# Forming the down projection's weight differences in another stage

## The chip, the cores and the metric

The kernel runs on one core of one Trainium2 chip. The metric is device time in microseconds (us) of one execution. Before the change it is 1341.98 us, the median of three runs (1338.4, 1341.98 and 1343.84).

In the profile PE is TensorE's matmuls and PEld its weight loads, DVE is VectorE, ACT is ScalarE, POOL is GpSimd. SP is the engine whose queue issues all of this kernel's DMAs, one behind the other (SPq in the rows).

## The reference, cut to what matters

One decoder layer over 1024 tokens and 16 meta tokens, model width 1024, all float32: a norm, an input projection that feeds four differential-attention heads and four HGRN heads in parallel, an output projection, a norm, and then a feed-forward part with a short convolution, which matters here:

```
def conv_ffn(a, w_up, conv_w, conv_b, w_down):
    u = a @ w_up                                   # 1024 -> 2 x 2816
    u = conv over 3 tokens, channel by channel, + conv_b
    gate, up = jnp.split(u, 2, axis=-1)
    return (jax.nn.gelu(gate, approximate=True) * up) @ w_down   # 2816 -> 1024
```

## The kernel before, in words

**Number format.** Every matmul operand in float32 is split into a rounded high part and a remainder (`split`, L146: the high part is a cast on ACT, the remainder a subtraction on DVE or POOL), and a product takes three matmuls (high by high, high by low, low by high). So each weight block costs a load, a cast and a subtraction before PE can use it.

**Stages.** The kernel is one unrolled program. After the first norm come the attention and HGRN heads: for each head `dense` (L742) computes input projections on PE while `attn` (L612) or `hgrn_head` (L395) runs beside it; `interleave` (L59) writes PE's order out by hand from costs per step. The stretches of this stage alternate: attention of a head beside the projections of the same head's HGRN (tiles `pi_hf`, `pi_hq`, `pi_hi`, `pi_hg`), then that head's HGRN beside the projections of the next head's attention (`pi_dq`, `pi_dk`, `pi_dv`). The order on PE is thus fixed; the order on the other engines and on SP is set at build time by a scheduler, in which an instruction earlier in the program goes first among those that it takes to be ready. `tc.issue_after(ins)` keeps what is issued inside the block behind `ins` on the engine of `ins`. At run time each engine works through its own queue in order and waits on semaphores.

**Up projection** (L1258 to L1371). The 2816 gate and 2816 up channels are worked off in 22 pairs of 128 (channel tiles, `ft` 0 to 21). From tile 1 on each pair is a two-by-two block product in seven products instead of eight, for two halves of the tokens (`unit`, p = 0 and 1, 258 and 256 columns per block). One tile has seven steps j = 0 to 6; in each, both units do 12 matmuls. The banks `pa`, `pb` and `pc` are accumulated into, evacuated and accumulated into again: step 1 fills `pb` and DVE adds it to `x1` to make `u2` (L1319, shown as `u<-pb`), step 3 adds further products into the same `pb`, so PE must wait there until that evacuation is done; DVE then makes `u3` (also `u<-pb`, L1325) and `uu`, step 5 goes into `pb` again. After step 6, `gated` (L1272) convolves gate and up (`conv`, L1263: one ACT instruction and two DVE instructions with three operands each, tiles `c`), takes gelu on ACT, multiplies on POOL and stores the rows to a DRAM scratch `gsc`. Beside this, `prep` (L1083) makes the weights of the next tile, seven steps ahead: loads `ra`, sums `ws` on POOL, high parts `uh` on ACT, remainders `ul` on DVE or POOL. Tile 0 is done plainly, in eight products (`plain_unit`).

**Down projection** (L1374 to L1547). It too is a block product in seven products, over 11 row blocks k. Four of the seven take differences of the weights of `w_down`: with blocks 11, 12, 21, 22 of rows k and k + 11 and of the two column halves, they are 12 - 11, 22 - 12, 22 - (12 - 11) and 21 - (22 - 12 + 11). They are formed ahead of time and kept in a DRAM scratch `tsc`, and `w_in` (L1394) reads them back for products 5, 6, 7 and 4, which are not the first two in the order (1, 2, 5, 6, 3, 7, 4).

**The differences** are made by `down_sums` (L184), a Python generator. For each of 11 values of k it loads four blocks `wd` (128x512, 256 KB each) on SP, then makes four subtractions on DVE in place, each followed by a store to `tsc`: 44 loads, 44 subtractions, 44 stores. Its blocks sit in six buffers of the pool `wsp`, which later also serves the output projection's weights. `dense` calls it once for each third of an input-projection tile (L749), so the work is spread over the attention and HGRN heads.

**The inputs of the down projection.** Rows of `gsc` come back in tiles `gi` (`g_in`, L1389), in the pool `dn` under the tag `gk` with four buffers; ACT and DVE split them into `gh` and `gl`, four buffers each. `ahead` (L1445) asks for them three steps ahead of use, and `sums5` (L1403) asks for rows of the second half. In program order the requests for `gk` buffers are: steps 0, 1, 2, 3 of product 1, then `sums5(0)`, then steps 4, 5 and so on. The pool `dn` is opened before tile 1 (L1359), so these loads can be issued during the up projection.

Of the kernel before, what the change touches and what calls it, by code (L numbers as in the profile page):

```python
# [9 lines left out]
F32 = mybir.dt.float32  # L10
# [3 lines left out]
ALU = mybir.AluOpType  # L14
# [3 lines left out]
P = 128  # L18
# [6 lines left out]
NF = DFF // P  # L25
# [6 lines left out]
WN = [258, 256]  # L32
C0 = [0, 514]
FA, FH, FO = 840, 800, 740


def start(i):
# [21 lines left out]
def interleave(dense, sides, fill, lead=0):  # L59
    sides = list(sides)  # L60
    live = True

    def feed(budget):
        nonlocal live
        while live and budget > 0:
            c = next(dense, False)
            if c is False:
                live = False
            elif c is None:
                return  # L70
            else:
                budget -= c

    feed(lead)
    while sides:
        for s in list(sides):
            c = next(s, False)
            if c is False:
                sides.remove(s)
                continue  # L80
            feed(fill * (c or 1))
    feed(1e12)
# [3 lines left out]
def layer_kernel(ctx: ExitStack, tc: tile.TileContext, x, meta, table, lbl, gpre, gpost, win,  # L86
# [3 lines left out]
    V, A = Ordered(tc, nc.vector, state), Ordered(tc, nc.scalar, state)  # L90
    G = Ordered(tc, nc.gpsimd, state)
    T, SY = nc.tensor, nc.sync

    def pool(name, bufs, side="left", space=None):
        kw = {"side": side} if space is None else {"space": space}
        cm = tc.tile_pool(name=name, bufs=bufs, reuse_waits="tile", **kw)
        return cm, cm.__enter__()
# [35 lines left out]
    tsc = dp.tile([4, DFF // 2, 512], F32, tag="tsc", name="tsc")  # L133
# [43 lines left out]
    ws_cm, wsp = pool("wdsums", 6)  # L177
# [3 lines left out]

    last_load = []

    def down_sums():  # L184
        def load(k):
            with tc.issue_after(last_load[-1].ins):
                for nm, kk, half in (("11", k, 0), ("12", k, 1), ("22", k + NF // 2, 1), ("21", k + NF // 2, 0)):
                    b[nm] = wsp.tile([P, 512], F32, tag="wd", name=f"wd{nm}_{k}")
                    SY.dma_start(b[nm], wdown[P * kk: P * (kk + 1), 512 * half: 512 * (half + 1)])

        b = {}
        load(0)
        yield
        yield
        for k in range(NF // 2):
            for j, d, p_, q_ in ((0, "11", "12", "11"), (2, "12", "22", "12"), (1, "22", "22", "11"), (3, "21", "21", "22")):
                V.tensor_tensor(b[d], b[p_], b[q_], op=ALU.subtract)
                with tc.issue_after(last_load[-1].ins):
                    SY.dma_start(tsc[j][P * k: P * (k + 1)], b[d])
                yield  # L200
            if k + 1 < NF // 2:
                load(k + 1)
                yield

    wd_sums = down_sums()
    at_p_cm, ap_ = pool("attn", 1, "right")
    z_cm, zp = pool("pre", 2, "right")

    def load_m(m, name, where=None, bufs=4):
        return [load_split(win[m][:, 512 * c: 512 * (c + 1)], f"{name}_{c}", where, bufs) for c in range(2)]  # L210

    def proj_group(g, parts, name, evac):
        b0, b1 = GROUPS[g]
        t0, t1 = start(b0), start(b1 - 1) + P
        n = t1 - t0
        pt = ps_in(f"pi_{name}_{g}")
        for k in range(KD):
            yield from proj_step(pt[:, :n], parts, k, t0, t1, lambda: evac(g, b0, b1, t0, t1, pt[:, :n]))
# [134 lines left out]
    def carried():  # L353
        tails = list(carry)
        carry.clear()
        return tails
# [34 lines left out]
    def flush():  # L391
        while late:
            to_nat(*late.pop(0))
# [345 lines left out]
                yield from values(i + 1)  # L739
        carry.append(pend.pop("tail"))  # L740

    def dense(tiles, preload=None, side=iter(())):  # L742
        parts = preload
        for idx, (m, name, evac) in enumerate(tiles):
            if parts is None:
                parts = load_m(m, name)
            nxt = load_m(tiles[idx + 1][0], tiles[idx + 1][1]) if idx + 1 < len(tiles) else None
            for g in range(3):
                next(side, None)  # L749
                for step, c in enumerate(proj_group(g, parts, name, evac)):  # L750
                    if step == 8:
                        flush()
                    yield c
            parts = nxt

    t_a, tiles = attn_in(0)
# [177 lines left out]

    for h in range(HEADS):
        t_h, tiles_h = hgrn_in(h)
        interleave(dense(tiles_h, None, wd_sums), [attn(h, t_a)] + carried(), FA, 1500)
        if h < HEADS - 1:
            t_a, tiles_a = attn_in(h + 1)
            interleave(dense(tiles_a, None, wd_sums), [hgrn_head(t_h)] + carried(), FH, 1500)  # L940

    close(at_cm)
    wo_cm, wop = pool("wo", 7)
# [127 lines left out]
    def load_raw4(ft):  # L1071
        raws.clear()
        for nm, m, c in (("11", ft, 0), ("22", ft + NF, 1), ("21", ft + NF, 0), ("12", ft, 1)):
            raws[nm] = swp.tile([P, 512], F32, tag="ra", name=f"ra{ft}_{nm}", bufs=5)
            with tc.issue_after(wo0_loaded.ins):
                SY.dma_start(raws[nm], wup[m][:, 512 * c: 512 * (c + 1)])
# [6 lines left out]
    def prep(q):  # L1083
        ft, j = divmod(q, 7)
        if ft >= NF or q in made:
            return
        if j == 0:
            load_raw4(ft)
            src = raws["11"]
            w_sum("1", raws["21"], raws["22"], ALU.add)  # L1090
        elif j == 1:
            src = w_sum("2", sums["1"], raws["11"], ALU.subtract)
        elif j == 2:
            src = sums["1"]
        elif j == 3:
            src = w_sum("3", raws["11"], raws["21"], ALU.subtract)
        elif j == 4:
            src = raws["12"]
        elif j == 5:
            src = raws["22"]  # L1100
        else:
            src = w_sum("4", raws["12"], sums["2"], ALU.subtract)
        where = swp if q % 2 else wp
        hi = where.tile([P, 512], F32R, tag="wh", name=f"uh{q}", bufs=4)
        lo = where.tile([P, 512], F32R, tag="wl", name=f"ul{q}", bufs=4)
        split(hi, lo, src, G if j % 2 == 0 and j else V)
        made[q] = (hi, lo)
# [150 lines left out]
    marks = {}  # L1258

    def outputs(ft, p):  # L1260
        return [xup.tile([P, 2 * WN[0]], F32, tag=t, name=f"{t}{ft}_{p}") for t in ("ug", "uu")]
# [36 lines left out]
    def unit(ft, p, bank):  # L1298
        n = WN[p]
        nm = f"{ft}_{p}"  # L1300
        ug, uu = outputs(ft, p)
        x1, u2, u3 = (xup.tile([P, WN[0]], F32, tag=t, name=f"{t}_{nm}")[:, :n] for t in ("x1", "u2", "u3"))

        def mm(j, pt, first):
            hi, lo = made[7 * ft + j]
            th, tl = tt[p][j]
            for k in range(4):
                s = slice(P * k, P * (k + 1))
                T.matmul(pt, hi[:, s], th[:, k], start=(first and k == 0), stop=False, skip_group_check=True)  # L1309
                T.matmul(pt, hi[:, s], tl[:, k], start=False, stop=False, skip_group_check=True)  # L1310
                T.matmul(pt, lo[:, s], th[:, k], start=False, stop=(k == 3), skip_group_check=True)  # L1311

        pa = bank(f"pa{nm}")[:, :n]
        mm(0, pa, True)
        A.copy(x1, pa)
        yield
        pb = bank(f"pb{nm}")[:, :n]
        mm(1, pb, True)
        marks[ft, p] = V.tensor_tensor(u2, pb, x1, op=ALU.add)  # L1319
        yield  # L1320
        pc = bank(f"pc{nm}")[:, :n]
        mm(2, pc, True)
        yield
        mm(3, pb, False)
        V.tensor_tensor(u3, pb, x1, op=ALU.add)  # L1325
        V.tensor_tensor(uu[:, n:2 * n], pc, u3, op=ALU.add)
        yield
        mm(4, pa, False)
        A.copy(ug[:, :n], pa)
        yield  # L1330
        mm(5, pb, False)
        V.tensor_tensor(uu[:, :n], pb, x1, op=ALU.add)
        yield
        mm(6, pc, False)
        V.tensor_tensor(ug[:, n:2 * n], pc, u2, op=ALU.add)
        gated(ft, p, ug, uu)
        yield

# [20 lines left out]
    dn_cm, dn = pool("down", 4, "right")  # L1359
    next(p0)  # L1360
    for j in range(4, 7):
        prep(7 + j)
    for ft in range(1, NF):
        units = [unit(ft, p, ps_b) for p in range(2)]
        for j in range(7):
            prep(7 * (ft + 1) + j)
            for u in units:
                next(u)
            if (ft, j) == (1, 1):
                with tc.issue_after(marks[1, 1].ins):  # L1370
                    next(p1)  # L1371
# [10 lines left out]
    x1 = ep.tile([P, 4, 512], F32, tag="e0", name="x1")  # L1382
    u2 = ep.tile([P, 4, 512], F32, tag="e1", name="u2")
# [230 lines left out]
```

## Time and profile before

| what | value |
|---|---|
| median of the runs | 1341.98 us |
| the profiled execution | 1336.17 us |
| its span, first to last instruction | 1334.1 us |
| granted TensorE clock | 0.995 |
| attention and HGRN heads | about 50 to 580 us of the span |
| up projection, tiles 1 to 21 | about 683 to 1108 us |
| down projection | from 1108 us |

The profile has a page and views that answer questions on the trace. The page gives busy time and share of each engine. The stretch view gives busy time of each engine between two times. The view of one tile or of one line gives count, shortest, median and longest duration, and first and last start. The view of waits gives, for an engine and what it wrote, which instruction or DMA it waited for: total, times, longest. The order in time gives start, length, engine, line, operation, output and inputs, shapes and count; in brackets stand the idle time of the engine before that instruction and what ended it. Names in rows are the program's tile names without numbers. Since V, A and G are wrapped in `Ordered`, their instructions all show line L53. Tiles written `wd`, `gi`, `gl`, `ul` and `u` are those described above.

### The profile page before, as it was taken

To read this page: it belongs to the slowest core of one execution; us is meant where nothing else is said; L and a number is where in the kernel's file an instruction comes from. 1 tells how busy PE (TensorE), PEld (TensorE's weight loads), DVE (VectorE), ACT (ScalarE), POOL (GpSimd) and SP (SyncE) were. 2 spreads that over 40 slices of the span, in tenths; PEclk is the share of its full clock that TensorE was granted. 3 is DMA by queue.
4 is the path that set the end of the run, shared out by engine and by line. 5 is a ranking of instruction groups with operands and counts; after the bars stand their busy time and mean duration, and the time that the engine had idled before them with its cause. 6 is when DMAs were issued, how large, how long until landed. Compare 5 with 4: busy or idle time off the path is not lost.

```text
span 1334.1 us, 26146 instructions
## 1 busy us (share of the span) xinstructions
PE 1287.9 (97%) x10172; PEld 1187.0 (89%) x10172; DVE 911.1 (68%) x1531; ACT 692.0 (52%) x1635; POOL 432.3 (32%) x340
## 2 busy tenths in 40 slices
PE   7999999999999999998998999999999999999997
PEld 6899899989999998677888999999999998878875
DVE  7675657475746574647797687787787776697586
ACT  8465356535654665246665445444445444454453
POOL 5211212121212110334055666666666630010121
PEclk9999999999999999999999999999999999999999
DMA  5331343144311223686412222223222226954253
GB/s 208 123 129 62 116 153 116 56 141 134 111 56 54 82 85 127 194 258 230 144 54 83 95 88 72 74 94 103 87 81 72 82 86 211 326 181 166 88 205 118
DMA packets 99425, 164.99 MB, mean 124 GB/s; under 512 B 10035, under 2 KB 34899, under 8 KB 99302
## 3 DMA queue, kind: packets, MB, share of 16 engines
q1 hardware_dynamic: 99302, 163.32, 35.9%
q8 instruction: 80, 1.31, 0.4%
q14 instruction: 43, 0.35, 0.1%
HBM read 122.65 MB, written 40.63 MB: 122 GB/s over the span
## 4 chain that ended last, share of the span: by engine, by line
PE 46%; DVE 7%; issue 3%; ACT 3%; DMA 2%; POOL 2%; SPq 0%; DVEq 0%; POOLq 0%; ACTq 0%
PE pd L1460 5%; PE pd L1461 5%; PE pd L1459 5%; PE pb L1309 4%; PE pb L1311 4%; PE pb L1310 4%; PE pc L1309 2%; PE pa L1309 2%; PE pa L1311 2%; PE pa L1310 2%; PE pc L1310 2%; PE pc L1311 2%; PE py L982 1%; PE py L980 1%; PE py L978 1%
## 5 line engine op out<-in xcount | busy, mean ns | idle before, releaser
L1309 PE MATMUL pb<-t,uh 128*128 128x258 f32 x504 | 142.9, 284 | 7.7 <-DVE u L53 7.7
L1310 PE MATMUL pb<-t,uh 128*128 128x258 f32 x504 | 141.7, 281 | 0.0
L1311 PE MATMUL pb<-t,ul 128*128 128x258 f32 x504 | 141.5, 281 | 0.0
L1460 PE MATMUL pd<-wl,gh 128*128 128x512 f32 x308 | 122.0, 396 | 0.3 <-DVE wl L53 0.2
L1459 PE MATMUL pd<-wh,gh 128*128 128x512 f32 x308 | 121.6, 395 | 0.0
L1461 PE MATMUL pd<-wh,gl 128*128 128x512 f32 x308 | 121.6, 395 | 0.0
L53 DVE SCALAR_TENSOR_TENSOR c<-uu,cwt,c 128x514 f32<-128x514 f32 (+1 forms) x88 | 97.1, 1104 | 20.6 <-ACT c L53 19.9
L1309 PEld LDWEIGHTS pb<-t,uh 128*128 128x128 f32 x504 | 95.4, 189 | 9.2 <-DVE u L53 8.9
L53 POOL TENSOR_TENSOR c<-c,c 128x514 f32<-128x514 f32 (+1 forms) x44 | 63.4, 1441 | 122.6 <-ACT c L53 118.5
L1310 PEld LDWEIGHTS pb<-t,uh 128*128 128x128 f32 x504 | 95.5, 189 | 0.0
L1311 PEld LDWEIGHTS pb<-t,ul 128*128 128x128 f32 x504 | 95.2, 189 | 0.0
L1309 PE MATMUL pa<-t,uh 128*128 128x258 f32 (+1 forms) x336 | 95.2, 283 | 0.0
L1311 PE MATMUL pa<-t,ul 128*128 128x258 f32 (+1 forms) x336 | 95.0, 283 | 0.0
L1310 PE MATMUL pa<-t,uh 128*128 128x258 f32 (+1 forms) x336 | 94.8, 282 | 0.0
L1309 PE MATMUL pc<-t,uh 128*128 128x258 f32 (+1 forms) x336 | 94.4, 281 | 0.0
L1310 PE MATMUL pc<-t,uh 128*128 128x258 f32 (+1 forms) x336 | 94.0, 280 | 0.0
L1311 PE MATMUL pc<-t,ul 128*128 128x258 f32 (+1 forms) x336 | 93.7, 279 | 0.0
L53 DVE SCALAR_TENSOR_TENSOR c<-ug,cwt,c 128x514 f32<-128x514 f32 (+1 forms) x88 | 86.7, 986 | 2.0 <-ACT c L53 1.4
L53 POOL TENSOR_TENSOR ul<-ws,uh 128x512 fp32r<-128x512 f32 x42 | 61.0, 1453 | 41.1 <-ACT uh L53 36.6
L1460 PEld LDWEIGHTS pd<-wl,gh 128*128 128x128 f32 x308 | 57.7, 187 | 15.5 <-DVE wl L53 1.6
L1459 PEld LDWEIGHTS pd<-wh,gh 128*128 128x128 f32 x308 | 57.7, 187 | 14.1
L1461 PEld LDWEIGHTS pd<-wh,gl 128*128 128x128 f32 x308 | 57.7, 187 | 14.0
(372 smaller groups left out, 4119.4 us busy)
## 6 DMA issues: line engine op xcount, KB each, us to landing
ra<-in_wup_dram SPq DMA_DIRECT2D x88, 256.0 KB, 2.6
mp<-msc SPq DMA_DIRECT2D x23, 512.0 KB, 6.3
wd<-in_wdown_dram SPq DMA_DIRECT2D x44, 256.0 KB, 4.4
tsc<-wd SPq DMA_DIRECT2D x44, 256.0 KB, 2.8
wi<-tsc SPq DMA_DIRECT2D x44, 256.0 KB, 2.8
gi<-gsc SPq DMA_DIRECT2D x33, 256.0 KB, 3.9
wi<-in_wdown_dram SPq DMA_DIRECT2D x33, 256.0 KB, 3.2
gsc<-c SPq DMA_DIRECT2D x22, 257.0 KB, 2.1
```

The costliest lines, as they stand in the source:

```text
L53: ins = call(*args, **kw)
L978: T.matmul(py[:r], mh, hi, start=(first and k == ks[0]), stop=False)
L980: T.matmul(py[:r], mh, lo, start=False, stop=False)
L982: T.matmul(py[:r], ml, hi, start=False, stop=(last and k == ks[-1]))
L1309: T.matmul(pt, hi[:, s], th[:, k], start=(first and k == 0), stop=False, skip_group_check=True)
L1310: T.matmul(pt, hi[:, s], tl[:, k], start=False, stop=False, skip_group_check=True)
L1311: T.matmul(pt, lo[:, s], th[:, k], start=False, stop=(k == 3), skip_group_check=True)
L1459: T.matmul(py, gh[:, s], wh, start=(k == 0 and pr not in (3, 7)), stop=False, skip_group_check=True)
L1460: T.matmul(py, gh[:, s], wl, start=False, stop=False, skip_group_check=True)
L1461: T.matmul(py, gl[:, s], wh, start=False, stop=(k == NH - 1), skip_group_check=True)
```

## The change

The generator moves from the attention stage into the up projection's loop, and `dense` loses its `side`. In the new place its blocks no longer lie in `wsp` but in the four buffers of the tag `gk`. It is called from channel tile 6 on (`SUMS`), after steps 1, 3, 5 and 6 of each tile, each time inside `issue_after` of the last evacuation traced so far (`marks["last"]`, set at each evacuation in `unit`), which is that of the second token half in this step. A call issues either the four loads of a k or one subtraction with its store: 55 calls in all. The arithmetic is the same.

```
+SUMS = 6
...
-        interleave(dense(tiles_h, None, wd_sums), [attn(h, t_a)] + carried(), FA, 1500)
+        interleave(dense(tiles_h), [attn(h, t_a)] + carried(), FA, 1500)
...
-            interleave(dense(tiles_a, None, wd_sums), [hgrn_head(t_h)] + carried(), FH, 1500)
+            interleave(dense(tiles_a), [hgrn_head(t_h)] + carried(), FH, 1500)
...
-        marks[ft, p] = V.tensor_tensor(u2, pb, x1, op=ALU.add)
+        marks[ft, p] = marks["last"] = V.tensor_tensor(u2, pb, x1, op=ALU.add)
...
-        V.tensor_tensor(uu[:, n:2 * n], pc, u3, op=ALU.add)
+        marks["last"] = V.tensor_tensor(uu[:, n:2 * n], pc, u3, op=ALU.add)
...
-        V.tensor_tensor(uu[:, :n], pb, x1, op=ALU.add)
+        marks["last"] = V.tensor_tensor(uu[:, :n], pb, x1, op=ALU.add)
...
-        V.tensor_tensor(ug[:, n:2 * n], pc, u2, op=ALU.add)
+        marks["last"] = V.tensor_tensor(ug[:, n:2 * n], pc, u2, op=ALU.add)
...
+    def down_sums():
+        for k in range(NF // 2):
+            b = {}
+            for nm, kk, half in (("11", k, 0), ("12", k, 1), ("22", k + NF // 2, 1), ("21", k + NF // 2, 0)):
+                b[nm] = dn.tile([P, 512], F32, tag="gk", name=f"wd{nm}_{k}")
+                SY.dma_start(b[nm], wdown[P * kk: P * (kk + 1), 512 * half: 512 * (half + 1)])
+            yield
+            for j, d, p_, q_ in ((0, "11", "12", "11"), (2, "12", "22", "12"), (1, "22", "22", "11"), (3, "21", "21", "22")):
+                V.tensor_tensor(b[d], b[p_], b[q_], op=ALU.subtract)
+                SY.dma_start(tsc[j][P * k: P * (k + 1)], b[d])
+                yield
+
+    wd_sums = down_sums()
...
+            if ft >= SUMS and j in (1, 3, 5, 6):
+                with tc.issue_after(marks["last"].ins):
+                    next(wd_sums, None)
```

More of the change, by code (lines that the diff above doesn't have):

```diff
@@ L182, in layer_kernel @@
     last_load = []
[L184 to L205, printed above, removed]
     at_p_cm, ap_ = pool("attn", 1, "right")
@@ L740, in attn, with dense @@
         carry.append(pend.pop("tail"))
-    def dense(tiles, preload=None, side=iter(())):
+    def dense(tiles, preload=None):
         parts = preload
@@ L748, in dense @@
             for g in range(3):
-                next(side, None)
                 for step, c in enumerate(proj_group(g, parts, name, evac)):
```

## The prediction

> **What bounds the kernel now.** The page comes first: span and engine shares.
>
> ```profile
> span 1334.1 us, 26146 instructions
> PE 1287.9 (97%) x10172; PEld 1187.0 (89%) x10172; DVE 911.1 (68%) x1531; ACT 692.0 (52%) x1635; POOL 432.3 (32%) x340
> ```
>
> TensorE (PE) is busy nearly all the time and no matmul is added or removed, so the change can only move PE's idle time. Two stages matter: attention beside HGRN, which loses the 44 differences, and the up projection, which gets them. The view of one tile (count, min/median/max ns, first and last start) places the old work; the waits of VectorE (DVE) add total, times, longest.
>
> ```profile
> L53 DVE TENSOR_TENSOR wd<-wd,wd x44: 673/693/1716, 56.4 to 349.8; 128x512 f32<-128x512 f32 x44
> DVE wd L53 <- DMA wd<-in_wdown_dram: 8.7, 10, 1.5
> ```
>
> This stage contains its own comparison, since the last difference is at 349.8 us while a third HGRN head follows without any. Its bounds are the first matmuls of tiles dq and hf of successive heads; the stretch view gives length, then PE, PEld, DVE, ACT and POOL busy (and count), clock, DMA share, GB/s.
>
> ```profile
> L224 PE MATMUL pi_dq<-ahi,wh_dq x24: 287/334/441, 137.8 to 154.7; 128*128 128x384 f32 x16, 128*128 128x272 f32 x8
> L224 PE MATMUL pi_hf<-ahi,wh_hf x24: 287/334/439, 191.3 to 205.8; 128*128 128x384 f32 x16, 128*128 128x272 f32 x8
> L224 PE MATMUL pi_dq<-ahi,wh_dq x24: 287/334/440, 267.1 to 285.3; 128*128 128x384 f32 x16, 128*128 128x272 f32 x8
> L224 PE MATMUL pi_hf<-ahi,wh_hf x24: 287/336/439, 321.1 to 335.7; 128*128 128x384 f32 x16, 128*128 128x272 f32 x8
> L224 PE MATMUL pi_dq<-ahi,wh_dq x24: 287/333/441, 397.2 to 412.2; 128*128 128x384 f32 x16, 128*128 128x272 f32 x8
> L224 PE MATMUL pi_hf<-ahi,wh_hf x24: 287/334/439, 447.9 to 462.4; 128*128 128x384 f32 x16, 128*128 128x272 f32 x8
> 137.80:191.30 53.50, 50.31 (x732) 47.52 (x732) 33.89 (x67) 23.84 (x67) 10.44 (x12) 1.00 0.36 120
> 191.30:267.10 75.80, 74.11 (x506) 71.21 (x506) 46.41 (x108) 45.95 (x139) 12.62 (x11) 1.00 0.33 110
> 267.10:321.10 54.00, 50.34 (x732) 47.50 (x732) 34.83 (x67) 23.81 (x67) 11.01 (x12) 1.00 0.35 118
> 321.10:397.20 76.10, 74.17 (x506) 71.20 (x505) 46.11 (x108) 45.98 (x139) 12.62 (x11) 1.00 0.33 107
> 397.20:447.90 50.70, 50.13 (x733) 47.44 (x732) 28.54 (x59) 23.83 (x67) 9.86 (x12) 1.00 0.18 57
> ```
>
> The same PE work with 67 DVE instructions takes 53.5 and 54.0 us, and with 59 (eight differences fewer) 50.7. In the up projection the stretch view shows PE full, DVE idle 24.1 of 105 us:
>
> ```profile
> 830.00:935.00 105.00, 105.00 (x888) 105.00 (x887) 80.89 (x118) 51.04 (x92) 64.99 (x46) 1.00 0.26 90
> ```
>
> **The change part by part.** *(a) Attention stage, removal.* Heads 0 and 1 should take what head 2 takes: 53.5 - 50.7 + 54.0 - 50.7 = 6.1 us. The order in time of DVE in head 0 shows the mechanism: a difference stood 1.48 us for its load ahead of the chain that PE's small matmuls need.
>
> ```profile
> 145.38 0.69 DVE L53 TENSOR_TENSOR wd<-wd,wd 128x512 f32<-128x512 f32 x1 [1.48 <-DMA wd<-in_wdown_dram]
> 146.58 1.42 DVE L53 TENSOR_TENSOR wd<-wd,wd 128x512 f32<-128x512 f32 x2
> ```
>
> The two attention stretches lose only 1.7 and 1.9 us of PE each, with attention's own waits among them; I take nothing, at most 3.6 together. Term: -6.1, bounds -9.7 and 0.
>
> *(b) Buffers of tag gk.* Before, the first four inputs gi of the down projection came into these four buffers during channel tiles 1 to 4, and PE paid. In the order in time the bracket is the idle before and its releaser:
>
> ```profile
> 701.99 0.69 DVE L53 TENSOR_TENSOR gl<-gi,gh 128x512 fp32r<-128x512 f32 x1 [3.50 <-ACT gh L53]
> 715.11 0.39 PE L1309 MATMUL pb<-t,uh 128*128 128x258 f32 x1 [3.30 <-DVE u L53]
> 719.28 0.62 ACT L53 CAST gh<-gi 128x512 fp32r<-128x512 f32 x1 [3.47 <-DMA gi<-gsc]
> 721.53 0.39 PE L1309 MATMUL pb<-t,uh 128*128 128x258 f32 x1 [0.45 <-DVE u L53]
> 742.36 0.39 PE L1309 MATMUL pb<-t,uh 128*128 128x258 f32 x1 [0.46 <-DVE u L53]
> 763.19 0.39 PE L1309 MATMUL pb<-t,uh 128*128 128x258 f32 x1 [0.42 <-DVE u L53]
> ```
>
> ACT stands in its queue for a load of rows just stored, DVE behind ACT, PE behind the evacuation u: 3.30 + 0.45 + 0.46 + 0.42 = 4.6 us. After the change the first four difference inputs are earlier in the program and need no stored rows, so I expect them to hold the buffers from the start, and gi to follow the last difference in tile 19. That buffers of one tag go in program order is supported by the next gi loads:
>
> ```profile
> 917.72 0.33 SPq L1277 DMA_DIRECT2D gsc<-c  x1
> 920.27 1.75 SPq L1391 DMA_DIRECT2D gi<-gsc  x4
> ```
>
> They leave only after tile 11's store, although rows of tiles 4 to 6 were there long before: the fifth request in program order (L1405) needs row 11. So -4.6 goes. The same four casts and differences come back in tiles 19 to 21, on rows stored long before; I charge 1.0, an estimate (two of the small waits above, since no load waits for a store there), bounds 0 and 4.6 (all returns).
>
> *(c) Up projection, addition.* Each call follows the evacuations of step j = 1, 3, 5 or 6. Of the 55 calls 11 load and 44 subtract, through j = 5 of tile 19. The order in time of DVE, PE and POOL decides which cost something:
>
> ```profile
> 876.33 0.74 DVE L53 TENSOR_TENSOR u<-pb,x 128x258 f32<-128x258 f32 x2
> 877.37 0.29 PE L1309 MATMUL pb<-t,uh 128*128 128x258 f32 x1
> 896.71 0.75 DVE L53 TENSOR_TENSOR u<-pb,x 128x258 f32<-128x258 f32 x2
> 897.30 0.29 PE L1309 MATMUL pb<-t,uh 128*128 128x258 f32 x1
> 898.10 0.69 DVE L53 TENSOR_TENSOR ul<-ws,uh 128x512 fp32r<-128x512 f32 x1 [0.65 <-ACT uh L53]
> 903.75 0.87 DVE L53 TENSOR_TENSOR ul<-ra,uh 128x512 fp32r<-128x512 f32 x1 [2.53 <-ACT uh L53]
> 906.01 0.76 DVE L53 SCALAR_TENSOR_TENSOR c<-uu,cwt,c 128x514 f32<-128x514 f32 x1 [0.95 <-ACT c L53]
> 908.07 1.63 POOL L53 TENSOR_TENSOR ws<-ra,ra 128x512 f32<-128x512 f32 x1
> 911.62 0.42 DVE L53 TENSOR_TENSOR ug<-pc,u 128x256 f32<-128x256 f32 x1
> 913.53 1.58 POOL L53 TENSOR_TENSOR c<-c,c 128x514 f32<-128x514 f32 x1 [3.83 <-ACT c L53]
> 916.19 0.75 DVE L53 TENSOR_TENSOR u<-pb,x 128x258 f32<-128x258 f32 x2
> L53 DVE TENSOR_TENSOR ul<-ra,uh 128x512 fp32r<-128x512 f32 x11 | 10.4, 942 | 12.7 <-ACT uh L53 12.7
> ```
>
> A difference at j = 1 lies in the idle 0.65, one at j = 3 in the idle 2.53: I cost both at nothing; without that cover their 22 would cost as those below. From 906.01 to the pair u at 916.19 DVE has no idle left, and the differences of j = 5 and 6 fall into this run, ahead of u. PE needs the first u of the pair: it ends about half the pair in, 897.09 against PE's start at 897.30 (margin 0.21), and 876.70 against 877.37 (0.67); the margins alternate by tile. One at j = 5 comes about a microsecond after 906.01, where GpSimd (POOL) works; I price it like ul, 0.94 on average. One at j = 6 comes behind 911.62, in POOL's idle 3.83; I price it at 0.69, wd's median. Loads take calls 0, 5, 10 and so on, which leaves 8 tiles with both (four of each margin), three with j = 5 alone (one at 0.21), three with j = 6 alone (two at 0.21). PE's stall: both, 4 x (1.63 - 0.21) + 4 x (1.63 - 0.67) = 9.5; j = 5, 0.73 + 2 x 0.27 = 1.3; j = 6, 2 x 0.48 + 0.02 = 1.0. Term +11.8. Below, it could be nothing (order otherwise); above, with 1.716, wd's slowest, for all 22, 22 x 1.716 - 7 x 0.21 - 7 x 0.67 = 31.6. I take the ul price since ul has the same form in this stage.
>
> The moved DMAs: 44 loads and 44 stores on SP.
>
> ```profile
> wd<-in_wdown_dram SPq DMA_DIRECT2D x44, 256.0 KB, 4.4
> tsc<-wd SPq DMA_DIRECT2D x44, 256.0 KB, 2.8
> ```
>
> A new buffer costs a store and a load, 2.8 + 4.4 = 7.2 us; from a fourth difference to the next first one lie at least three steps of (897.30 - 877.37) / 7 = 2.85, so 8.5. Nothing to wait for, narrowly: were the load late by 1 us, the conv chain and u behind it on DVE would be too. On SP the weight loads ra stand behind these issues; a DMA share of 0.26 leaves room. Cost nothing.
>
> *Sum:* -6.1 - 4.6 + 1.0 + 11.8 = +2.1 us. The profiled execution took 1336.17 us (span 1334.1 and 2.1 around it), so 1338.3; the shown median is 1341.98, against which I forecast **1344.1**.
>
> **The rivals.** *Slower: the port.* GpSimd is busy 65 of 105 us here against 10 to 11 of 54 in the HGRN stretches, and ul's mean is 942 ns where the one at 898.10 took 0.69. If each difference in the run costs more, the term grows by 22 us for each us of price: at 1.52 and 0.94 for j = 5 and 6 (mean 1.23) it is 22 x 1.23 - 6.2 = 20.9, and the time 1341.98 - 9.7 + 20.9 = 1353.2. It is slower by 0.5% (6.7 us) from a mean of 1.03. Against it: the idle 3.83 of POOL when j = 6 comes. The Trainium skill, SBUF — State Buffer, section "Who interferes with whom", has the rule: a DVE instruction with two SBUF inputs and a GpSimd instruction that reads SBUF exclude each other for the whole instruction. By it a difference behind a GpSimd instruction pays most of that one too, and the sum would be nearer 1353; wd's median of 693 with a maximum of 1716 agrees that it happens, seldom in the stage with little GpSimd work.
>
> *Faster: the run takes nothing.* If the differences reach DVE only in its idle places (24.1 us of 105 are there), (c) is 0 and the time 1332.3. Against it: j = 5 and 6 come before the next u in the program.
>
> *It doesn't do what it says: gi keeps its buffers.* If gi is still fetched in tiles 1 to 4, (b) is 0: 1341.98 - 6.1 + 11.8 = 1347.7, and differences delayed beyond tile 19 would be next. The four loads at 920.27 speak against.
>
> **How the numbers follow.** Forecast 0.50, port 0.27, faster 0.16, gi kept 0.07. Half a per cent is about what a measurement of this kernel can tell from no change: 1335.3 to 1348.7. Forecast gives 0.46 within, 0.01 faster, 0.03 slower; the port 0.27 slower; the third 0.16 faster; the last 0.06 within, 0.01 slower: faster 0.17, same 0.52, slower 0.31. The range takes in both rivals' times with about a microsecond beyond: 1331 to 1355; the forecast's own is 1338 to 1350.
>
> **What would show it.** HGRN heads 0 and 1 at 50.7 us each; no gl in tiles 1 to 4 and none of the four PE waits there; PE waits on u at step 3 of tiles 7 to 20, some 0.3 to 1.4 us each, in alternation; wd at j = 1 and 3 in DVE's idle. It would be wrong if wd at j = 5 or 6 stands behind the next u, if DVE waits for wd loads (the spacing above), or if ACT waits for ra because SP stands at a wd issue.

## The result, and the profile after

The kernel after takes **1337.24 us** (median of 22 runs, 1331.78 to 1340.71), the kernel before 1340.45 us (22 runs, 1336.26 to 1347.05). The ratio is 0.9974 with a 95% interval of 0.9963 to 0.9985: faster by 0.26%, about 3.5 us by this ratio (the medians alone differ by 3.2). Forecast was 1344.1 us, slower by 2.1. The time lies in the stated range (1331 to 1355) and within the half per cent that the prediction called no change, but below the forecast's own range (1338 to 1350) and on the other side of no change: the sign was wrong.

First the page of the kernel after, span and engine shares. Without the generator at its top the kernel's lines have moved: L53 is L54 here, PE's L1309 is L1287, the loads of `gi` at L1391 are at L1386.

```profile
span 1336.4 us, 26161 instructions
PE 1292.8 (97%) x10172; PEld 1191.7 (89%) x10172; DVE 929.2 (70%) x1531; ACT 691.5 (52%) x1635; POOL 453.7 (34%) x340
```

Each of the five engines has as many instructions in this row as before, but DVE is busy 18.1 us longer (911.1 before) and POOL 21.4 us longer (432.3). The profiled execution took 1338.2 us, 2.0 more than that of before (1336.17), while the median is 3.2 less. So the first pair of traces shows where time moved, but not the whole sum; two more executions of before come below (number 8).

**Attention beside HGRN.** The first and the last of the six bounds (tile view of the kernel after), then its stretches between them (length, PE, PEld, DVE, ACT, POOL busy with counts, clock, DMA share, GB/s):

```profile
L203 PE MATMUL pi_dq<-ahi,wh_dq x24: 287/333/440, 137.3 to 152.3; 128*128 128x384 f32 x16, 128*128 128x272 f32 x8
...
L203 PE MATMUL pi_hf<-ahi,wh_hf x24: 287/334/439, 439.9 to 454.4; 128*128 128x384 f32 x16, 128*128 128x272 f32 x8
```

```profile
137.30:188.00 50.70, 50.13 (x733) 47.43 (x733) 28.55 (x59) 23.86 (x67) 9.86 (x12) 1.00 0.16 49
188.00:263.20 75.20, 73.54 (x505) 71.22 (x504) 42.41 (x100) 46.53 (x138) 12.57 (x11) 1.00 0.16 48
263.20:313.90 50.70, 50.13 (x733) 47.43 (x732) 28.55 (x59) 23.83 (x67) 9.86 (x12) 1.00 0.16 48
313.90:389.20 75.30, 73.64 (x505) 71.32 (x505) 42.45 (x100) 46.63 (x139) 12.55 (x11) 1.00 0.17 48
389.20:439.90 50.70, 50.13 (x733) 47.43 (x733) 28.55 (x59) 23.85 (x67) 9.86 (x12) 1.00 0.19 56
```

All three HGRN heads take 50.7 us now, as forecast, and the attention stretches also give 0.6 and 0.8 us, which I had priced at nothing. The projections that follow head 2's HGRN start 8.0 us earlier (447.9 before).

**Up projection.** One row each: the differences in their new place, and the time that PE waited for the evacuation `u` there (total, times, longest):

```profile
L54 DVE TENSOR_TENSOR wd<-wd,wd x44: 676/1382/1577, 786.5 to 1063.2; 128x512 f32<-128x512 f32 x44
PE pb L1287 <- DVE u L54: 10.1, 11, 4.4
```

A difference takes 1382 ns in the median instead of 693. The four waits that the prediction showed ahead of tile 5 are gone. In their place PE waits in the tiles with differences, and once for 4.4 us. The order in time around that one wait, in tiles 19 and 20:

```profile
1054.69 0.32 SPq L1386 DMA_DIRECT2D gi<-gsc  x1
1058.00 0.62 ACT L54 CAST gh<-gi 128x512 fp32r<-128x512 f32 x1 [3.36 <-DMA gi<-gsc]
1058.65 1.65 DVE L54 TENSOR_TENSOR gl<-gi,gh 128x512 fp32r<-128x512 f32 x1 [1.30 <-ACT gh L54]
1060.64 0.95 SPq L1386 DMA_DIRECT2D gi<-gsc  x2
...
1064.87 0.62 ACT L54 CAST gh<-gi 128x512 fp32r<-128x512 f32 x1 [2.71 <-DMA gi<-gsc]
...
1067.45 1.86 DVE L54 SCALAR_TENSOR_TENSOR c<-uu,cwt,c 128x510 f32<-128x510 f32 x1 [2.58 <-POOL ul L54]
...
1075.10 0.41 DVE L54 TENSOR_TENSOR u<-pb,x 128x258 f32<-128x258 f32 x1
1075.44 1.71 DVE L54 TENSOR_TENSOR gl<-gi,gh 128x512 fp32r<-128x512 f32 x1
1075.57 0.58 PE L1287 MATMUL pb<-t,uh 128*128 128x258 f32 x1 [4.37 <-DVE u L54]
1075.95 0.42 PE L1288 MATMUL pb<-t,uh 128*128 128x258 f32 x1
```

Read the brackets on ACT: it stood 3.36 and 2.71 us for loads issued only a few microseconds before. Those rows had been stored long ago; what was late is the issue of the load, behind the last differences, against the cast's place in ACT's queue. The conv on DVE came 2.58 us late behind that, and with it `u` and PE. (Its bracket names POOL's `ul`; the conv's own ACT instruction, behind the second of the two casts, ran from 1066.54 to 1067.35, 0.1 us before the conv.) After the wait the matmuls start 0.21 to 0.22 us apart instead of 0.12, and the granted clock of 1070 to 1080 us is 0.72.

The start of the same matmul, counted from the first instruction of the span, after minus before, in the first pair of traces and with a second execution of after (against the same execution of before):

| where | first pair | second execution of after |
|---|---|---|
| end of head 2's HGRN | -8.0 | -8.2 |
| start of the up projection | -9.4 | -8.6 |
| tile 6, before the first difference | -15.0 | -15.1 |
| tile 19 | -6.0 | -6.2 |
| start of the down projection | +1.5 | +0.4 |
| last matmul | +1.8 | -0.1 |

So the four terms are there: the attention stage about -8 to -9, the end of the `gi` waits -5.6 to -6.5, the differences +9, the return of `gi` +7.

### The profile page after: what moved, and what is told of

It is laid out like the page before. It is cut to its first block, busy times and chain, and to the rows that moved or that the text cites. A ratio compares the mean times of both kernels' runs of the same rounds, so it can differ in the third digit from the quotient of the medians.

```text
span 1336.4 us, 26161 instructions
## 1 busy us (share of the span) xinstructions
PE 1292.8 (97%) x10172; PEld 1191.7 (89%) x10172; DVE 929.2 (70%) x1531; ACT 691.5 (52%) x1635; POOL 453.7 (34%) x340
## 4 chain that ended last, share of the span: by engine, by line
PE 43%; DVE 11%; DMA 4%; issue 3%; ACT 3%; POOL 1%; SPq 0%; DVEq 0%; POOLq 0%; ACTq 0%
PE pd L1455 5%; PE pd L1456 4%; PE pd L1454 4%; PE pb L1287 4%; PE pb L1288 4%; PE pb L1289 4%; DVE c L54 3%; PE pa L1287 2%; PE pa L1289 2%; PE pa L1288 2%; PE pc L1287 2%; PE pc L1288 2%; PE pc L1289 2%; DMA gi<-gsc 1%; DMA xh<-in_x_dram 1%
## 5 line engine op out<-in xcount | busy, mean ns | idle before, releaser
L1287 PE MATMUL pb<-t,uh 128*128 128x258 f32 x504 | 145.8, 289 | 12.2 <-DVE u L54 12.1
L1288 PE MATMUL pb<-t,uh 128*128 128x258 f32 x504 | 143.5, 285 | 0.0
L54 POOL TENSOR_TENSOR c<-c,c 128x514 f32<-128x514 f32 (+1 forms) x44 | 74.7, 1698 | 120.9 <-ACT c L54 106.8
L1287 PEld LDWEIGHTS pb<-t,uh 128*128 128x128 f32 x504 | 97.2, 193 | 15.4 <-DVE u L54 15.3
L54 DVE SCALAR_TENSOR_TENSOR c<-uu,cwt,c 128x514 f32<-128x514 f32 (+1 forms) x88 | 88.3, 1012 | 22.8 <-ACT c L54 19.9
L1288 PEld LDWEIGHTS pb<-t,uh 128*128 128x128 f32 x504 | 97.5, 193 | 0.0
L1289 PEld LDWEIGHTS pb<-t,ul 128*128 128x128 f32 x504 | 97.1, 193 | 0.0
L1287 PE MATMUL pa<-t,uh 128*128 128x258 f32 (+1 forms) x336 | 95.3, 284 | 0.0
L1287 PE MATMUL pc<-t,uh 128*128 128x258 f32 (+1 forms) x336 | 94.4, 281 | 0.0
L54 DVE SCALAR_TENSOR_TENSOR c<-ug,cwt,c 128x514 f32<-128x514 f32 (+1 forms) x88 | 88.2, 1002 | 1.5 <-ACT c L54 1.4
L54 ACT CAST uh<-ra 128x512 fp32r<-128x512 f32 x67 | 41.0, 616 | 68.9 <-PE pb L1288 50.4
L54 POOL TENSOR_TENSOR ul<-ws,uh 128x512 fp32r<-128x512 f32 x42 | 63.8, 1520 | 28.1 <-ACT uh L54 28.1
```

Source lines behind the costliest of these rows:

```text
L54: ins = call(*args, **kw)
```

## Experiments

**Theory:** these four terms make the result; the return of `gi` can be had back by asking for those loads later, and the differences cost time only in the run of DVE ahead of `u` (j = 5 and 6), about their plain 0.69 us less PE's margin. **Rival, the port:** collisions with GpSimd set their price, wherever they stand. **Rival, noise:** the attention stage gave little, 0 to 4 us, and the rest is run-to-run difference.

Numbers 1, 2, 3 and 5 were measured on one chip and 4, 6 and 7 on another, each beside the kernel before (medians 1341.52 and 1340.63 us); so they are compared by their ratios to it.

**1. No differences at all.** The 44 loads, subtractions and stores are left out, and products 5, 6, 7 and 4 read plain blocks of the weights, with as many bytes.

```
-                    next(wd_sums, None)
+                pass
...
-            SY.dma_start(t, tsc[(5, 6, 7, 4).index(pr)][P * k: P * (k + 1)])
+            SY.dma_start(t, wdown[P * k: P * (k + 1), :512])
```

> The changed kernel without the 44 differences, their loads and their stores; products 5, 6, 7 and 4 of the down projection read plain blocks of its weights in their place, so they compute something else. Theory (the attention stage gives its time back): about 8.1 us faster than before (median 1340.45), so 1332.3, with HGRN stretches of 50.7 us and the four PE waits of tiles 1 to 4 back as before. Rival (the two profiled executions differ in the granted clock, 0.995 and 0.991, and the stage gives back less): 0 to 4 us faster, 1336 to 1340.

Measured: 1329.54 us, ratio to before 0.9914 (0.9887 to 0.9940). Without the differences `gi` comes back to tiles 1 to 4, as before, so this is the attention stage alone: -11.5 us, at least 8, more than the 8.1 expected here and the 6.1 of the prediction. The rival of noise falls. Loads, subtractions and stores are left out together, so the run doesn't tell which of the three the stage paid for.

**2. The same, with `gi` late.** Beside the edit above, the loads of `gi` are tied behind tile 20's second store:

```
-        SY.dma_start(gsc[P * ft: P * (ft + 1), C0[p]:C0[p] + 2 * WN[p] - 2], cg)
+        marks["gsc", ft, p] = SY.dma_start(gsc[P * ft: P * (ft + 1), C0[p]:C0[p] + 2 * WN[p] - 2], cg)
...
-        SY.dma_start(t, g_src(k, half))
+        with tc.issue_after(marks["gsc", 20, 1].ins):
+            SY.dma_start(t, g_src(k, half))
```

> The kernel no_sums with the loads gi issued on SP only behind the store of tile 20's second half, so that none can come into the first tiles. Theory (gi in tiles 1 to 4 costs what the waits and the shift of the whole stage show, 4.6 to 6.9 us): 5 to 7 us faster than no_sums, about 1326. Rival (what is taken away there comes back when the down projection starts with its first casts still to be made): within 2 us of no_sums.

Measured: 1322.26 us, ratio 0.9861 (0.9836 to 0.9886); 7.1 us below the one before, give or take 5. This is the stage with neither of the two costs.

**3. The kernel after, with `gi` late** (the second diff alone).

> The changed kernel with the loads gi issued on SP only behind the store of tile 20's second half; the arithmetic is the changed kernel's. Theory (the return of gi in tile 20, a PE wait of 4.65 us and the lower clock behind it, took most of the gain): 4 to 7 us faster than the changed kernel, so 1330 to 1333. Rival (that wait is the profiled execution's alone, or it moves to the start of the down projection): within 2 us of the changed kernel, 1335 to 1339.

Measured: 1332.0 us, ratio 0.9931 (0.9908 to 0.9954). In this kernel's up projection PE's waits are

```profile
PE pb L1287 <- DVE u L54: 7.6, 12, 1.4
```

The 4.4 is gone from the list, whose longest is 1.4. Against the kernel after this gives back 0.43%, 5.8 us: the price of the return of `gi`, an edit of two lines that beats both kernels. Against number 2 it gives the price of the differences with their loads and stores, +9.4 us, give or take 5. By the starts of the same matmuls in these two traces, all of it (10.0 us) lies between tile 6 and the start of the down projection.

**4. The kernel before, with `gi` late.** The second diff, on the kernel before.

> The kernel before with one edit: the loads gi are issued on SP only behind the store of tile 20's second half. Theory (gi in tiles 1 to 4 costs 6 to 7 us wherever the differences are formed): 6 to 7 us faster than before, ratio near 0.995. Rival (the gain seen between no_sums and no_sums_late belongs to kernels without differences in the attention stage): within 2 us of before.

Measured: 1335.69 us, ratio 0.9965 (0.9948 to 0.9981): -4.7 us. This measures the waits of tiles 1 to 4 with the differences in their old place. That is less than the 6 to 7 expected, which the interval (2.5 to 7.0) still takes in. At least about as much as the whole change brings (0.9974) is to be had without moving a difference. Number 2 against this one is a second measure of the attention stage: -13.9 us, give or take 4.

**5. Differences only at j = 1 and 3**, one and two, from tile 2 on; `gi` as in the kernel after.

```
-SUMS = 6
+SUMS = 2
...
-            if ft >= SUMS and j in (1, 3, 5, 6):
+            for _ in range((1, 3, 3).count(j) if ft >= SUMS else 0):
```

> The changed kernel with one call after step 1 and two after step 3 of each tile, from tile 2 on, instead of one after steps 1, 3, 5 and 6 from tile 6 on. Theory of the prediction (only a difference in the run of conv instructions before the next u costs PE): the waits of PE at step 3 go, about 7 to 9 us, so 1328 to 1330. Rival (VectorE and GpSimd exclude each other, and step 3 is where GpSimd makes its sums, so the time comes back as later conv instructions meet GpSimd): the waits stay at half or more, 1333 to 1340.

Measured: 1338.74 us, ratio 0.9986 (0.9972 to 1.0001). The theory missed here, and the time lies in the rival's range; PE's waits for `u` are 15.3 us, against 10.1 in the kernel after. The order in time of DVE in one tile, and PE's first matmul of the next step 3:

```profile
895.40 3.27 DVE L54 TENSOR_TENSOR wd<-wd,wd 128x512 f32<-128x512 f32 x2
898.60 1.78 DVE L54 TENSOR_TENSOR ul<-ra,uh 128x512 fp32r<-128x512 f32 x1
...
901.66 0.75 DVE L54 SCALAR_TENSOR_TENSOR c<-uu,cwt,c 128x514 f32<-128x514 f32 x1 [0.95 <-ACT c L54]
...
912.22 0.39 PE L1287 MATMUL pb<-t,uh 128*128 128x258 f32 x1 [1.42 <-DVE u L54]
```

Two differences in a row take 3.27 us beside GpSimd, more than the idle 2.53 that I had counted at j = 3, so `ul`, `uu`, the conv and the next `u` are late. This is tile 11. In tiles 2, 7, 12 and 17 the call after step 1 issues loads, and the pair meets GpSimd less. In tile 7:

```profile
813.14 2.44 DVE L54 TENSOR_TENSOR wd<-wd,wd 128x512 f32<-128x512 f32 x2
815.76 1.52 DVE L54 TENSOR_TENSOR ul<-ra,uh 128x512 fp32r<-128x512 f32 x1 [0.18 <-ACT uh L54]
```

Here the pair fits, 0.18 us of idle is left, and PE has no wait in tile 8; nor has it behind the other three. So the idle place takes two differences of 2.44 us together, not of 3.27: what GpSimd adds decides there, and the rival is right in that much.

**6. One at j = 1 and one at j = 3**, from tile 1 on, one more at j = 5 in tiles 20 and 21; the four loads are issued in the call of the first difference (a `yield` less), and `gi` is late.

```
-SUMS = 6
+SUMS = 1
...
-            yield
...
-            if ft >= SUMS and j in (1, 3, 5, 6):
+            if ft >= SUMS and (j in (1, 3) or (ft >= 20 and j == 5)):
```

> The kernel late_gi with the differences placed otherwise: one after step 1 and one after step 3 of each tile from tile 1 on, and one more after step 5 in tiles 20 and 21; the loads of a k go out with the call of its first difference, so 44 calls. Theory (one at step 3, even at the 1.57 us that it takes beside GpSimd, fits the idle 2.53 us there, and one at step 1 has the distance of over 3 us to PE's step 5): the waits at step 3 go, 1 to 3 us over no_sums_late (1322.3), so 1323 to 1326. Rival (collisions with GpSimd lengthen what follows wherever the difference stands): like late_gi, 1330 to 1333.

Measured: **1327.68 us**, ratio 0.9895 (0.9877 to 0.9913), the fastest of the kernels that compute the reference, between the two ranges expected: 1.7 us above the theory's, 2.3 below the rival's. DVE in one tile, and all waits of PE from 683 to 1120 us (the down projection starts at 1097):

```profile
906.53 1.40 DVE L54 TENSOR_TENSOR wd<-wd,wd 128x512 f32<-128x512 f32 x1
...
911.14 1.57 DVE L54 TENSOR_TENSOR wd<-wd,wd 128x512 f32<-128x512 f32 x1
912.96 1.45 DVE L54 TENSOR_TENSOR ul<-ra,uh 128x512 fp32r<-128x512 f32 x1 [0.25 <-ACT uh L54]
...
915.70 0.75 DVE L54 SCALAR_TENSOR_TENSOR c<-uu,cwt,c 128x514 f32<-128x514 f32 x1 [0.95 <-ACT c L54]
```

```profile
PE pb L1287 <- DVE u L54: 4.1, 2, 2.1
PE pd L1456 <- DVE gl L54: 2.1, 1, 2.1
```

The differences collide with GpSimd as hard as any (1.40 and 1.57 us), but the conv begins, as in the kernel before, after its own 0.95 of waiting for ACT: the idle ahead of it took the whole. Both waits for `u` lie before 692 us, in tile 1, where number 2 too has two, of 2.5 us; from tile 2 on there is none. The new wait of 2.1 us, in the down projection, is the price of differences that last until 1096 us, with `gi` behind them. By the starts of the same matmuls, against the trace of number 2, tile 1 is 3.1 us longer (1.0 of it ahead of the first difference; the first, at 683.32 us, then stands in the conv run of tile 0, ahead of `u`), the first steps of the down projection 3.1 us, and tiles 2 to 21 are as long within 0.2. These two places make 6.2 us in the traces, where the ratios differ by 4.6. In tiles 2 to 21 neither the differences nor their loads and stores cost anything.

**7. All in the run**: one at j = 5 and two at j = 6, from tile 2 on, `gi` late.

```
-            if ft >= SUMS and j in (1, 3, 5, 6):
+            for _ in range((5, 6, 6).count(j) if ft >= SUMS else 0):
```

> The kernel late_gi with one call after step 5 and two after step 6 of each tile, from tile 2 on. Theory (in the run of conv instructions each difference costs PE its plain 0.69 us, less the margin once in a tile): 44 x 0.69 - 18 x 0.44 = 22 us over no_sums_late (1322.3), so 1343 to 1346. Rival (the cost goes by how many differences the stage has, not by their places): about 9 us over it, near late_gi's 1332.

Measured: 1361.92 us, ratio 1.0144 (1.0117 to 1.0171), in the theory's direction and larger than it said. The differences of this kernel, and PE's waits there:

```profile
L54 DVE TENSOR_TENSOR wd<-wd,wd x44: 675/685/1533, 715.8 to 1105.0; 128x512 f32<-128x512 f32 x44
PE pb L1287 <- DVE u L54: 28.2, 19, 2.8
```

Here most differences take their plain 685 ns, and they cost the most; in number 6 they take 1412 ns in the median and cost nothing at step 3. So a price can't be read from the length of the instruction. It doesn't follow that they don't collide: 18 of the 44 lie inside a GpSimd instruction (`c`) of about 2.2 us, where it takes 1.58 in the rows of before. So what the collisions add to the price in this run is not separated; it may be why the cost is larger than the plain lengths said. About 8 us of the median lie beyond the profiled execution (1354.03) and are not placed; the two runs near 1354 us have a granted clock of 0.993, the four of 1361 to 1365 us 0.985 to 0.990.

**8. Where the sum of the first traces differs from the medians.** The kernel before twice more, and the kernel after once, unchanged, each for another profiled execution.

> The kernel before, unchanged, for a second profiled execution; the first took 1336.17 us where the median of its runs is 1340.5. Theory: the first one lost less to low granted clocks than most do; then this one takes 1338 to 1345 us, every HGRN stretch and every up projection tile is as long as in the first within 0.3 us, and the surplus lies in stretches of 10 us with a granted clock under 1. Rival: the differences beside attention stand longer for their loads in some executions; then the HGRN and attention stretches of heads 0 and 1 are longer than 53.5, 75.8, 54.0 and 76.1 us, by 2 us or more in all, at a clock of 1.00.

> As for the second execution of the kernel before: a third one, so that the stretches have three values each. Theory: 1338 to 1345 us, stretches the same within 0.3 us at a clock of 1.00. Rival: stretches of heads 0 and 1 differ by 2 us or more in all.

> The kernel after, unchanged, for a second profiled execution; the first took 1338.2 us where the median of its runs is 1337.2. Both theories: 1333 to 1340 us, HGRN stretches of 50.7 us and a stall of 4 to 5 us ahead of step 3 in tile 20 again; surplus or saving only where the granted clock differs.

Measured: before 1345.19 and 1341.89 us, after 1336.25 us, one execution each. In the second execution of after, the wait in tile 20 is 3.5 us, shorter than the 4 to 5 expected. Stretches of the second and the third execution of before, with the bounds used above:

```profile
138.00:193.80 55.80, 52.00 (x732) 49.06 (x731) 33.91 (x67) 23.81 (x67) 10.31 (x12) 0.97 0.35 114
193.80:270.30 76.50, 74.34 (x505) 71.31 (x505) 46.40 (x108) 45.87 (x139) 12.61 (x11) 1.00 0.34 109
270.30:324.00 53.70, 50.60 (x732) 47.63 (x732) 34.82 (x67) 23.79 (x67) 10.82 (x12) 1.00 0.37 118
324.00:401.50 77.50, 74.48 (x506) 71.19 (x505) 46.07 (x108) 45.90 (x139) 12.60 (x11) 1.00 0.32 105
```

```profile
140.30:194.10 53.80, 50.25 (x733) 47.47 (x732) 33.87 (x67) 23.83 (x67) 10.47 (x13) 1.00 0.37 119
194.10:271.00 76.90, 74.40 (x505) 71.24 (x505) 46.41 (x108) 45.98 (x139) 12.63 (x11) 1.00 0.33 109
271.00:326.10 55.10, 51.82 (x733) 48.95 (x732) 34.89 (x67) 23.79 (x67) 10.97 (x12) 0.97 0.35 115
326.10:402.90 76.80, 74.40 (x506) 71.17 (x505) 46.07 (x108) 45.96 (x139) 12.61 (x11) 1.00 0.33 106
```

From head 0's `pi_dq` to head 2's the kernel before takes 259.4, 263.5 and 262.6 us in its three executions, the kernel after 251.9 and 252.0. So the theory (stretches the same, only clocks differ) fails, and its rival holds for about half of the 4.1 and 3.2 us that this stage takes more than in the first execution: the attention stretches are longer by 2.1 and 1.8 us together at a clock of 1.00, and one HGRN stretch each at 0.97 adds 2.3 and 1.1. The rows of DVE's waits for `wd` fit: the longest is 1.5 in the first execution, 2.6 and 2.3 in these. The first trace, on which the prediction was built, was the mildest of the three in this stage; with the differences gone the stage has the same length in both executions. The removal is worth 7.5, 11.6 and 10.7 us here; the last two lie in what number 1 measures (8 to 15), the first just below it. The spans of the two executions are 9.1 and 5.8 us above the first one's; the 5.0 and 2.6 us that this stage doesn't hold are not explained. These three executions ran on a third chip, and the record doesn't say on which the first two ran; so execution and chip are not told apart.

## Why the prediction was wrong

| term | forecast | in the traces | by runs |
|---|---|---|---|
| (a) attention stage | -6.1 | -7.5, -11.6, -10.7 | -11.5 (number 1), -13.9 (2 against 4) |
| (b) `gi` gone from tiles 1 to 4 | -4.6 | -5.6 to -6.5 | -4.7 (4), -7.1 (2 against 1) |
| return of `gi` | +1.0 | +7.5, +6.6 | +5.8 (after against 3) |
| (c) differences | +11.8 | +9.0, +8.9 | +9.4 (3 against 2) |

By runs, with number 1 for (a) and number 2 for (b), the terms add up to -3.4, the measured -3.5 but for rounding; they must, since each is the step from one kernel to the next. What stands beside them on its own is number 4 for (a) and (b), and the traces for the others.

All four effects came, and all four with the sign that was forecast; three of the terms were mis-sized, the return of `gi` for a wrong reason, and together they turned the sign.

- *(a) "Term: -6.1, bounds -9.7 and 0"* is the step that decided. Its rows were those of one execution, and the waits for `wd` loads vary from one to the next. By runs it measured 11.5 and 13.9 us, beyond the bound of 9.7, which the first interval (8 to 15) still takes in. With -11.5 in its place the prediction's sum is -3.3, a faster kernel. The attention stretches, "I take nothing", give 0.6 to 2.2 us each.
- *Return of `gi`, "I charge 1.0 ... since no load waits for a store there".* True, and beside the point: the load leaves only when a buffer is free behind the last differences, and ACT's queue reaches the cast before it has landed. The upper bound (4.6, all returns) was too low as well; it left out the matmuls at half their pace after the wait.
- *(c) +11.8, measured 9.* The places were right: PE waited on `u` at step 3, in tiles 7, 8, 11 to 13 and 16 to 18 of the 7 to 20 foreseen, up to 1.15 us with one of 4.4 beside, and the difference at j = 1 and at j = 3 cost nothing, one each (number 6). The prices were not: DVE in tile 10, its first row that of before and the others of the kernel after, with one row of POOL, and PE behind it:

```profile
886.62 0.75 DVE L53 SCALAR_TENSOR_TENSOR c<-uu,cwt,c 128x514 f32<-128x514 f32 x1 [0.95 <-ACT c L53]
...
874.63 0.76 DVE L54 SCALAR_TENSOR_TENSOR c<-uu,cwt,c 128x514 f32<-128x514 f32 x1 [0.95 <-ACT c L54]
...
875.63 1.46 DVE L54 TENSOR_TENSOR wd<-wd,wd 128x512 f32<-128x512 f32 x1
877.02 0.41 DVE L54 TENSOR_TENSOR ug<-pc,u 128x258 f32<-128x258 f32 x1
877.35 2.10 DVE L54 SCALAR_TENSOR_TENSOR c<-uu,cwt,c 128x514 f32<-128x514 f32 x2
...
881.96 2.25 POOL L54 TENSOR_TENSOR c<-c,c 128x514 f32<-128x514 f32 x1 [3.72 <-DMA ra<-in_wup_dram]
882.36 0.68 DVE L54 TENSOR_TENSOR wd<-wd,wd 128x512 f32<-128x512 f32 x1
882.96 1.79 DVE L54 SCALAR_TENSOR_TENSOR c<-ug,cwt,c 128x510 f32<-128x510 f32 x1
...
885.88 0.74 DVE L54 TENSOR_TENSOR u<-pb,x 128x258 f32<-128x258 f32 x2
...
886.35 0.39 PE L1287 MATMUL pb<-t,uh 128*128 128x258 f32 x1 [0.85 <-DVE u L54]
```

The two differences take 1.46 and 0.68 us, 2.14 together, and yet the run from the first conv instruction to `u` is only 885.88 - 874.63 = 11.25 us long, where the same tile before the change has 896.71 - 886.62 = 10.09. They add 1.16, against the 1.63 that the prediction charged. Over tiles 6 to 18 both add 1.04 to 1.16 us to this run, the one at j = 6 alone 0.50 to 0.60 (charged 0.69), the one at j = 5 alone 0.44 and 0.55 (charged 0.94). The one at j = 5 stands beside a GpSimd instruction (`ul`) that a conv instruction met before, and the eight conv instructions of the run take 7.7 us together instead of 8.3. The page of the kernel after has that for all tiles:

```profile
L54 DVE SCALAR_TENSOR_TENSOR c<-uu,cwt,c 128x514 f32<-128x514 f32 (+1 forms) x88 | 88.3, 1012 | 22.8 <-ACT c L54 19.9
```

Before, the 88 took 97.1 us (mean 1104 ns): 8.8 us less, while the differences got longer.
- *The port.* The rows show the lock that the rival named, and on either side: most differences that begin 0.3 to 0.5 us into a GpSimd instruction take 1.38 to 1.58 us instead of 0.68, while the one at 882.36, where a conv instruction was running when GpSimd's began, takes its 0.68 and the GpSimd instruction around it 2.25 instead of 1.58. The Trainium skill, SBUF — State Buffer, section "Who interferes with whom", says that the two exclude each other for the whole instruction, and the trace agrees. In the kernel after it did not bring the rival's price (+20.9), since the added collisions in part stand in place of those of the conv instructions. Where a pair outgrew the idle place, in number 5, it did set the time.
- *`wd` loads:* no wait of DVE for them, as forecast. *`gi` keeps its buffers:* it did not; the first `gi` load leaves at 1054.69.
- *The sum* was made against one execution and laid on the median of three (1341.98, where 22 runs give 1340.45). In that pair of traces it is right by chance (+2.1 forecast, +1.8 at the last matmul); over the runs it is -3.5.

What stays open: how much of the longer stretches in the attention stage is the wait for `wd` itself, how much the lower clock of two of them (0.97), and how much the loads and stores, which no run takes out alone.

## What to carry to other kernels

An engine's idle place takes what fits with its collisions counted, so spread moved work as one instruction for each idle place rather than in groups (a pair fitted here at 2.44 us and not at 3.27), and price it by how much later the next awaited instruction comes, not by its own length. When a buffer changes its owner, look for what now asks for it last: a load issued late in front of an in-order queue stalls everything behind it, whether or not its data was ready. A stage with waits for DMA can differ from execution to execution (here by up to 4.1 us in three, and by 0.1 in two once the loads were gone); take such a term from more than one trace before betting on its sign.

## What the runs showed of the hardware

- After PE's 4.4 us wait some 24 matmuls started 0.21 us apart instead of 0.12, at a granted clock of 0.72 in those 10 us (0.66 in the second execution of after). The same came behind a 2.7 us wait of PE in the second execution of before (0.88 from 170 to 180 us), and in its third behind a wait of 1.75 us at 287.8 us (0.86 from 290 to 300 us). A wait of 1.8 us at 284 us of its first execution, and one of 2.4 us at 178 us of its third, had none of it (1.00). So the length of the single wait does not tell which.
- The collision can lengthen POOL's instruction instead of DVE's, as the 2.25 us above show. The page of the kernel after has

```profile
L54 POOL TENSOR_TENSOR c<-c,c 128x514 f32<-128x514 f32 (+1 forms) x44 | 74.7, 1698 | 120.9 <-ACT c L54 106.8
```

where before the mean was 1441 ns: 11.3 of POOL's 21.4 us more lie in this group. Eight of the 44 take about 2.24 us, each around a difference of 0.68.
